# Two early one-row stores cut to a quarter of a row each, in a DMA-bound RMSNorm kernel

## The chip, the cores and the metric

The kernel runs on one core of a Trainium2 chip. The metric is the device time of one execution in microseconds. Before the change it is 162.1 us (median of 3 runs, 161.9 to 162.29).

## The reference

```python
x: (16, 1024, 512) float32, gamma: (512,) float32 (ones)
rms = np.sqrt(np.mean(x ** 2, axis=-1, keepdims=True) + 1e-5)
return (x / rms * gamma).astype(np.float32)
```

x has 33.55 MB and the output as many. Nothing can be left out: 67.1 MB cross between HBM (the chip's main memory) and SBUF (the core's working memory, in 128 partitions).

## The kernel before

The 16,384 rows are four tiles of 128 partitions x 32 rows. A partition's 32 rows lie one after the other in HBM (64 KB), so that a DMA is 128 contiguous runs, one per partition. Three buffers of a tile's size ("slots") hold tiles 0, 1, 2; tile 3 goes into slot 0 again. ScalarE (ACT) squares rows, VectorE (DVE) reduces some of them and applies scale and gamma in place. Every load and store of x and the output goes through one queue, issued by SyncE (SP) in the order of the program:

```python
def load(t, slot, r0, r1):
    nc.sync.dma_start(out=slots[slot][:, r0:r1], in_=xv[t][:, r0:r1])

def store(t, slot, r0, r1):
    nc.sync.dma_start(out=ov[t][:, r0:r1], in_=slots[slot][:, r0:r1])

load(0, 0, 0, 8)
load(0, 0, 8, 32)
# ... gamma to all partitions; row_stats (squares, sum, 1/rms) and apply (x * rstd * gamma), 8 rows at a time

def transfers(t, g):          # called after rows g..g+8 of tile t are applied
    if (t, g) == (0, 0):
        store(0, 0, 0, 1)     # early store 1: row 0, 2,048 B per partition
        load(1, 1, 0, 32)
        load(2, 2, 0, 16)
        store(0, 0, 1, 2)     # early store 2: row 1
        load(2, 2, 16, 32)
    elif (t, g) == (0, 24):
        store(0, 0, 2, 16)    # the "first big store"
        store(0, 0, 16, 32)
        load(3, 0, 0, 16)
        load(3, 0, 16, 32)
    # ... stores of tiles 1, 2, and of tile 3 in two halves
```

The statistics of a group are computed one group ahead of its application.

## Time and profile before

| | before |
|---|---|
| time, median | 162.1 us |
| span of the profiled run | 160.4 us |
| DVE, ACT busy | 76%, 50% |
| DMA queue, share of 16 engines' span | 97.7% |
| first packet of x starts, last packet ends | 1.74, 159.25 us |

These are lines of the page of the kernel before: the span, the busy times, the DMA share of 40 slices of the span, the count of packets (one packet is one partition's run; besides, each of the 15 DMAs of x and the output ends on every engine with a completion packet of 4 B, 240 of the 241 under 512 B), and the queue of all x and output traffic.

```profile
span 160.4 us, 410 instructions
PE 2.0 (1%) x2; PEld 0.5 (0%) x2; DVE 122.6 (76%) x163; ACT 80.1 (50%) x162; POOL 0.2 (0%) x4
...
DMA  5999999699699999999999999998998998999993
...
DMA packets 2164, 67.13 MB, mean 419 GB/s; under 512 B 241, under 2 KB 241, under 8 KB 498
...
q1 hardware_dynamic: 2160, 67.11, 97.7%
```

The DMA engines are the limit. No compute engine is near its own. The two slices with a 6 are no holes: long packets are counted where they start, and the packet records show the queue served in the order of issue without a gap. The 257 packets of at least 2 KB but under 8 KB are the 2 x 128 of the early stores and gamma.

The chain of waits names DVE, and this is the reading to be careful with. Here are its shares, and then the waits of the queue that issues the DMAs.

```profile
DVE 67%; DMA 13%; ACT 7%; issue 2%; DVEq 0%; SPq 0%
...
SPq L45 <- DVE slot L88: 97.9, 7, 29.8
SPq L42 <- DMA out_dram<-slot: 31.3, 2, 21.9
```

The last store is issued when DVE ends its last row, so the chain goes from there back through DVE. But an issued store stands in line. The packet records say that the last store, issued at 146.25 us, has its first packet at 148.28, behind the store before it. DVE is 2.0 us early even there.

### The profile page before, as it was taken

How to read it: one execution, taken by the hardware profiler on the slowest of the kernel's cores; microseconds unless marked ns; L12 is line 12 of the kernel's file. 1: busy time of each engine (PE TensorE's matmuls, PEld its weight loads, DVE VectorE, ACT ScalarE, POOL GpSimd, SP SyncE). 2: the span in 40 equal slices, each digit the busy share in tenths (PEclk: the TensorE clock that was granted, in tenths of full speed). 3: DMA queues.
4: the chain of work that ended last, by engine and by line, in shares of the span. 5: the costliest groups of instructions: out<-in, count | busy, mean ns of one | idle time of the engine just before them, and what ended most of it. 6: DMA issues, size and time to landing. Idle time of an engine off the chain costs nothing.

```text
span 160.4 us, 410 instructions
## 1 busy us (share of the span) xinstructions
PE 2.0 (1%) x2; PEld 0.5 (0%) x2; DVE 122.6 (76%) x163; ACT 80.1 (50%) x162; POOL 0.2 (0%) x4
## 2 busy tenths in 40 slices
PE   4000000000000000000000000000000000000000
PEld 1000000000000000000000000000000000000000
DVE  0100928999999519999999999999999999994000
ACT  3098039990390999996900950079609940000000
POOL 0000000000000000000000000000000000000000
DMA  5999999699699999999999999998998998999993
GB/s 197 523 392 392 466 449 523 261 523 523 262 402 387 455 458 418 453 415 466 409 392 498 409 400 507 409 507 376 425 507 360 441 507 360 417 400 441 449 417 147
DMA packets 2164, 67.13 MB, mean 419 GB/s; under 512 B 241, under 2 KB 241, under 8 KB 498
## 3 DMA queue, kind: packets, MB, share of 16 engines
q1 hardware_dynamic: 2160, 67.11, 97.7%
q14 instruction: 2, 0.02, 0.0%
q10 hardware_dynamic: 2, 0.00, 0.0%
HBM read 33.56 MB, written 33.55 MB: 418 GB/s over the span
## 4 chain that ended last, share of the span: by engine, by line
DVE 67%; DMA 13%; ACT 7%; issue 2%; DVEq 0%; SPq 0%
DVE slot L88 48%; DVE ss L71 18%; DMA slot<-in_x_dram 13%; ACT sq_scratch L76 3%; ACT sq L70 3%; DVE rstd L83 1%; DVEq L154 0%; ACT rms L82 0%; SPq L42 0%
## 5 line engine op out<-in xcount | busy, mean ns | idle before, releaser
L88 DVE SCALAR_TENSOR_TENSOR slot<-slot,rstd,gamma_b 128x512 f32<-128x512 f32 x128 | 85.8, 738 | 0.1
L76 ACT ACTIVATE sq_scratch<-slot 128x512 f32<-128x512 f32 x64 | 40.0, 625 | 10.0 <-DMA slot<-in_x_dram 8.7
L70 ACT ACTIVATE sq<-slot 128x2048 f32<-128x2048 f32 x16 | 29.8, 1864 | 18.6 <-DVE ss L71 11.5
L71 DVE TENSOR_REDUCE ss<-sq 128x4 f32<-128x2048 f32 x16 | 35.9, 2274 | 3.4 <-ACT sq L70 3.4
L82 ACT ACTIVATE rms<-ss,eps_t 128x8 f32<-128x8 f32 x16 | 4.6, 297 | 25.9 <-DVE ss L71 25.7
L83 DVE RECIPROCAL rstd<-rms 128x8 f32<-128x8 f32 x16 | 3.1, 193 | 16.1 <-ACT rms L82 16.1
L76 ACT ACTIVATION_READ_ACCUMULATOR sq_scratch<-slot 128x1 f32 x64 | 11.9, 186 | 0.0
L57 DVE COPY gamma_b<-sq 128x512 f32<-128x512 f32 x1 | 0.7, 691 | 3.3 <-PE sq L55 3.3
L55 PE MATMUL sq<-gamma_row,ones_col 1*128 1x512 f32 x2 | 2.0, 1122 | 2.2 <-DMA gamma_row<-in_gamma_dram 2.2
L76 ACT ACT_TABLE_LOAD x1 | 1.3, 1283 | 1.3 <-PEq L143 1.3
L82 ACT ACT_TABLE_LOAD x1 | 1.3, 1283 | 0.0
L53 DVE MEMSET ones_col<- 1x128 f32 x1 | 0.2, 165 | 0.8 <-PEq L143 0.8
L55 PEld LDWEIGHTS sq<-gamma_row,ones_col 1*128 1x128 f32 x2 | 0.5, 306 | 2.2 <-issue 2.2
L143 POOL MEMSET const-bfloat16-1.0<- 128x1 bf16 x1 | 0.1, 101 | 0.0
L143 POOL MEMSET const-uint8-127<- 128x1 uint8 x1 | 0.1, 101 | 0.0
L143 POOL MEMSET const-float32-0.0<- 128x1 f32 x1 | 0.1, 98 | 0.2 <-issue 0.2
L143 POOL MEMSET const-float32-1.0<- 128x1 f32 x1 | 0.1, 98 | 0.0
L60 DVE MEMSET eps_t<- 128x1 f32 x1 | 0.1, 59 | 0.0
## 6 DMA issues: line engine op xcount, KB each, us to landing
slot<-in_x_dram SPq DMA_DIRECT2D x4, 4096.0 KB, 27.6
out_dram<-slot SPq DMA_DIRECT2D x3, 4096.0 KB, 18.8
slot<-in_x_dram SPq DMA_DIRECT2D x1, 6144.0 KB, 21.5
out_dram<-slot SPq DMA_DIRECT2D x1, 3584.0 KB
slot<-in_x_dram SPq DMA_DIRECT2D x1, 2048.0 KB, 7.2
out_dram<-slot SPq DMA_DIRECT2D x2, 256.0 KB, 21.3
out_dram<-slot SPq DMA_DIRECT2D x2, 29.8
gamma_row<-in_gamma_dram ACTq DMA_DIRECT2D x1, 2.0 KB
```

Source lines behind the costliest of these rows:

```text
L53: nc.vector.memset(ones_col, 1.0)
L55: nc.tensor.matmul(gamma_psum[:, 0], ones_col, gamma_row, start=True, stop=True)
L57: nc.vector.tensor_copy(out=gamma_b, in_=gamma_psum[:, 0])
L60: nc.vector.memset(eps_t, eps)
L70: nc.scalar.activation(out=sq, in_=slots[slot][:, g + h : g + h + H, :], func=AF.Square)
L71: nc.vector.tensor_reduce(out=ss[:, h : h + H], in_=sq, axis=mybir.AxisListType.X, op=OP.add)
L76: nc.scalar.activation(out=sq_scratch, in_=slots[slot][:, g + r, :], func=AF.Square, accum_out=ss[:, r : r + 1],)
L82: nc.scalar.activation(out=rms, in_=ss, func=AF.Sqrt, bias=eps_t, scale=1.0 / D)
L83: nc.vector.reciprocal(out=rstd, in_=rms)
L88: nc.vector.scalar_tensor_tensor(out=slots[slot][:, g + r, :], in0=slots[slot][:, g + r, :], scalar=rstd[:, r : r + 1], in1=gamma_b, op0=O ...
L143: nc = _bacc.Bacc("TRN2", target_bir_lowering=False, num_devices=1)
```

## The change

The idea: the two early stores are made as small as a quarter of a row (512 B per partition), so that they take less of the queue from the loads behind them. The first big store takes the rest. Nothing else changes.

```diff
+    def store_elements(t, slot, e0, e1):
+        nc.sync.dma_start(
+            out=ov[t].rearrange("p r d -> p (r d)")[:, e0:e1],
+            in_=slots[slot][:].rearrange("p r d -> p (r d)")[:, e0:e1],
+        )
...
-            store(0, 0, 0, 1)
+            store_elements(0, 0, 0, D // 4)
             load(1, 1, 0, 32)
             load(2, 2, 0, 16)
-            store(0, 0, 1, 2)
+            store_elements(0, 0, D // 4, D // 2)
             load(2, 2, 16, 32)
...
-            store(0, 0, 2, 16)
+            store_elements(0, 0, D // 2, 16 * D)
```

## The prediction

> **What bounds the kernel now.** The 16 DMA engines. The page puts the DMA queue at 97.7% of the engines' span, 67.1 MB at 419 GB/s. The trace's packet records show one queue, served in issue order, with no hole: the first packet of x starts at 1.74 us, the last ends at 159.25, the span is 160.4. The longest packets (65,536 B, 2.418 us) give 27.1 GB/s per engine, at which its 4.19 MB take 154.8 us: the 157.5 us of DMA hold some 2.7 us of overhead. The Trainium skill ("DMA: Bandwidth & Descriptors", Specifications) puts the fabric ceiling at 435 GB/s; 16 x 27.1 = 434 agrees.
>
> The chain of waits names DVE for 67%, because the last store is issued when DVE ends its last row (146.25 us in the timeline). But its first packet starts only at 148.27, behind the store before it. DVE is 2.0 us ahead of the queue here, 3.4 at tile 2's store, 7.5 or more elsewhere.
>
> **What the change does.** No instruction is added or removed. The two early stores go from 128 packets of 2,048 B each to 128 of 512 B; the 393 KB taken from them go into the first big store of slot 0 (28,672 to 31,744 B per partition). A 2,048 B packet took 84 ns, against 75.6 at the rate above: 8 ns of overhead. If that is fixed, a 512 B packet takes an estimated 27 ns; each engine has 16: 0.43 us in place of 1.34. The big store's packets grow by 0.113 us, 8 per engine: +0.91. The sum is zero. If a 512 B write costs as much as a 2,048 B one (the same skill section puts the least size for line rate at 512 B, so this is its edge), the sum is +0.9; I expect 0.0 to +0.3.
>
> What moves: tile 1 lands some 0.45 us earlier (42.7 to 42.3), tile 2's second half 0.9 earlier, until the big store gives it back near 72 us. ACT waits 3.3 us for tile 1, but then again for DVE's reductions to free PSUM (to 52.0 us), so this is absorbed. The second early store now depends on row 0 alone; it was issued at 17.99, after row 1 was done, so this buys nothing.
>
> **On the critical path:** only packet overhead, near zero. I predict 162.1 us, with 8 chances in 10 for 161.5 to 163.0. Faster by over 2%: 0.01; within 2%: 0.95; slower by over 2%: 0.04. (2% is 3.2 us.)
>
> **What would show it.** Right: packets under 2 KB rise by 256, those under 8 KB stay; DMA share stays at 97 to 98%; 512 B packets take 25 to 40 ns; tile 1 lands 0.3 to 0.6 us earlier; from the store of slot 0's second half on, all is within 0.5 us of before. Wrong in cost: 512 B packets take 80 ns or more. Wrong in hiding: a hole in the DMA queue before a late store.
>
> **What would make it wrong.** ACT and DVE interleave row groups (single-row and four-row squares alternate), so the order seems chosen at build time, perhaps from assumed DMA times. Another order could end DVE later: by over 2 us to show, by over 5 to cost 2%. DVE stands idle 5.4 us before 59.6; an order could add to that. I give a changed order 40%, a harmful one 8%. An earlier DVE end cannot help: the queue is full.

## More of the kernel before

The order of instructions on ACT and DVE is chosen when the program is built.

## The result, and the profile after

After: 162.7 us median (162.47 to 162.97, 4 runs); before, with the runs of that round, 162.12 us (161.9 to 162.29, 4 runs). The ratio is 1.0038, 95% interval 1.0014 to 1.0062. A ratio is the mean time of one kernel's fast runs over that of the other's of the same rounds, so it is not quite the ratio of the medians. By the 2% rule the two are the same; but the two sets of four do not overlap, and the change costs about 0.6 us.

The same lines of the page of the kernel after:

```profile
span 161.1 us, 411 instructions
PE 2.0 (1%) x2; PEld 0.5 (0%) x2; DVE 122.6 (76%) x163; ACT 80.1 (50%) x162; POOL 0.2 (0%) x4
...
DMA  5999999969999999999999999899899799799992
...
DMA packets 2164, 67.13 MB, mean 417 GB/s; under 512 B 241, under 2 KB 497, under 8 KB 498
...
q1 hardware_dynamic: 2160, 67.11, 97.5%
...
DVE 64%; DMA 13%; ACT 10%; issue 2%; DVEq 0%; SPq 0%
```

Compute is the same to a tenth of a microsecond, the packets are as many, and 256 of them have moved under 2 KB. Apart from line numbers, the sizes of three DMAs and one more semaphore wait on DVE (at 114.98 us; with it the page counts 411 instructions, and DVE still ends 0.18 us sooner), the built programs have the same instructions in the same order on every engine. The DMA queue is as full as before and 0.7 us longer.

Where do the 0.7 us arise? The DMA view of a narrow window, taken at the issue of one DMA, has a line for that DMA (and at times one for its neighbour): its size, where it is given, and the time from issue to landing. These lines are tile 1's load, the second half of tile 2's, the store of the second half of tile 0, and the last store. First before (line 2 was issued at 18.51, line 3 at 49.81, line 4 at 146.25 us):

```profile
slot<-in_x_dram SPq DMA_DIRECT2D x1, 25.7
...
slot<-in_x_dram SPq DMA_DIRECT2D x1, 4096.0 KB, 44.9
...
out_dram<-slot SPq DMA_DIRECT2D x1, 4096.0 KB, 32.1
...
out_dram<-slot SPq DMA_DIRECT2D x1, 4096.0 KB, 13.3
```

Then after (issued at 18.50, 49.62, 146.07 us):

```profile
slot<-in_x_dram SPq DMA_DIRECT2D x1, 25.0
...
slot<-in_x_dram SPq DMA_DIRECT2D x1, 4096.0 KB, 44.4
...
out_dram<-slot SPq DMA_DIRECT2D x1, 4096.0 KB, 32.8
...
out_dram<-slot SPq DMA_DIRECT2D x1, 4096.0 KB, 14.2
```

Tile 1 lands 0.7 us earlier (predicted: 0.3 to 0.6). The second half of tile 2, which should have been 0.9 us early, is only 0.5 early. Then the big store takes back its 0.9 us, as it had to, and everything behind it is late by 0.5 us or more. So time was gained ahead of the first early store and more was lost in the loads of tile 2.

The DMA view of two windows finds it. Only packets that *start* in the window are counted, with their full duration, so a share can exceed 100%; share x window x 16 / packets is the mean duration of a packet. First before, 19.8 to 20.4 us (the last packet of each engine ahead of early store 1), then 58.2 to 61.5 us (the last packets of tile 2's load, ahead of the first big store):

```profile
q1 hardware_dynamic: 16, 0.79, 350.2%
...
q1 hardware_dynamic: 46, 1.51, 106.2%
```

Then after, the same two windows:

```profile
q1 hardware_dynamic: 16, 0.79, 302.9%
...
q1 hardware_dynamic: 32, 1.05, 101.2%
```

In the first window the 49,152 B packets took 2.10 us before (3.502 x 0.6 us) and 1.82 after; such a packet takes 1.815 us when undisturbed. In the second the 32,768 B packets took 1.22 us before (1.062 x 3.3 x 16 / 46) and 1.67 after; undisturbed, 1.213. So *loads* become slow just ahead of a store, and the change has moved this from the early stores to the big one.

To compare runs I sum, over the packets of a stretch, the duration less size / 27.1 GB/s, and divide by 16. The result is the lost time per engine. A small store's own packets are included: 128 of 2,048 or of 512 B have 8 ns each over the rate, which is 0.06 us per engine. The last two columns are the mean and the latest start of the last store's 16 completion packets.

| trace | lost up to early store 1's end | from there up to early store 2's | up to the big store's start | sum | queue's end, mean | slowest engine |
|---|---|---|---|---|---|---|
| before | 0.38 us | 0.45 | 0.08 | 0.90 | 158.34 us | 159.24 |
| after | 0.08 | 0.15 | 0.97 | 1.20 | 158.74 | 159.98 |

The first column starts at the end of the first load; the second leaves out tile 1's load (0.03 to 0.04 us). The sum rises by 0.30 us. The queue's mean end rises by 0.40 (0.05 of it is there when the first load ends), and the slowest engine, which sets the span, by 0.74: its lag on the mean is 1.24 us in place of 0.90.

The table leaves out one more place. Ahead of the store of tile 1, where the queue turns from loads to stores again, the last packets of tile 3's load are slow too. Here are the 16 packets that start at 98.7 to 99.9 us before, the 16 at 98.9 to 100.1 us after, and the last one of the slowest engine after (100.1 to 100.2 us):

```profile
q1 hardware_dynamic: 16, 0.52, 112.2%
...
q1 hardware_dynamic: 16, 0.52, 110.5%
...
q1 hardware_dynamic: 1, 0.03, 112.9%
```

Their means are 1.35 and 1.33 us in place of 1.213, and the single one took 1.81 us (1.129 x 0.1 x 16). This second loss is smaller, some 0.03 to 0.19 us per engine over all traces, but uneven: by the completion packets, the lag of the slowest engine grew from 0.65 to 0.92 us there before, and from 0.79 to 1.25 after (in the repeats below from 0.58 to 0.83 and from 0.71 to 1.05).

### The profile page after: what moved, and what is told of

Read it like the earlier page. It is cut to its first block, busy times and chain, and to the rows that moved or that the text cites. A ratio compares the mean times of both kernels' runs of the same rounds, so it can differ in the third digit from the quotient of the medians.

```text
span 161.1 us, 411 instructions
## 1 busy us (share of the span) xinstructions
PE 2.0 (1%) x2; PEld 0.5 (0%) x2; DVE 122.6 (76%) x163; ACT 80.1 (50%) x162; POOL 0.2 (0%) x4
## 3 DMA queue, kind: packets, MB, share of 16 engines
q1 hardware_dynamic: 2160, 67.11, 97.5%
## 4 chain that ended last, share of the span: by engine, by line
DVE 64%; DMA 13%; ACT 10%; issue 2%; DVEq 0%; SPq 0%
DVE slot L94 45%; DVE ss L77 18%; DMA slot<-in_x_dram 13%; ACT sq_scratch L82 5%; ACT sq L76 5%; DVE rstd L89 1%; ACT rms L88 1%; DVEq L160 0%; SPq L42 0%; DVEq L94 0%
## 5 line engine op out<-in xcount | busy, mean ns | idle before, releaser
L76 ACT ACTIVATE sq<-slot 128x2048 f32<-128x2048 f32 x16 | 29.8, 1864 | 18.9 <-DVE ss L77 12.0
```

Source lines behind the costliest of these rows:

```text
L76: nc.scalar.activation(out=sq, in_=slots[slot][:, g + h : g + h + H, :], func=AF.Square)
```

## The experiments

Eleven kernels ran. Theory A: the changed big store itself (where its rows start, or its length) makes the loads ahead of it slow. Theory B: the early stores used to take this stall in advance, and became too small for it. Each kernel keeps the order of instructions on DVE and ACT unless said otherwise, and each gave the right result. The diffs are against the changed kernel where not said otherwise.

### The two kernels once more

No edit.

> Control: the changed kernel once more. If the 0.6 us are real and come from the last two load packets of each engine ahead of the first big store (they took about 1.75 and 1.6 us in place of 1.213 between 58 and 62 us), the time is 162.5 to 162.9 us and the trace shows the same slow packets, some 0.9 us per engine, in the same place. Rival: those slow packets were a chance of one execution; then they are gone or elsewhere, and the time is not tied to them.

> Control: the kernel before, profiled once more. If the trace's stalls belong to the program, its load packets are slow just ahead of the two early stores again (0.3 to 0.4 us per engine each, near 20 and 49.5 us) and not ahead of the first big store (under 0.1 us); time 162.1 +- 0.2. Rival (chance): the stalls lie elsewhere or have other sizes.

After: 162.68 us (162.25 to 163.05, 6 runs). Before, as a kernel of its own: 162.00 us (161.87 to 162.16, 6 runs). The shared runs of before on this chip scattered more (162.2, 161.85 to 163.53, 11 runs), so that the ratio of after is 1.0021 with an interval of 0.9992 to 1.005. Over all rounds the 43 runs of before have a median of 162.13, the 10 of after 162.68. I take the cost as 0.5 to 0.6 us; the interval of the second comparison alone would not show it.

The stalls came again. After: 0.12, 0.10, 0.92 us, with the slow packets at the same place. Before: 0.51, 0.10, 0.36. So in before the stall at early store 1 came both times, but the second part was paid at early store 2 in one execution and ahead of the big store in the other; there I had expected under 0.1. The sum is steady: 0.97 (0.90 before), and 1.15 (1.20) after.

### The big store as it was, with one small early store

```diff
-            store_elements(0, 0, D // 4, D // 2)
+            store_elements(0, 0, D // 4, 2 * D)
-            store_elements(0, 0, D // 2, 16 * D)
+            store_elements(0, 0, 2 * D, 16 * D)
```

> First early store 512 B per partition as in the change, second takes the rest of rows 0 and 1 (3,584 B), so that the big store has the 28,672 B at byte 4,096 that it had before. Theory A (the changed big store itself, its start or length, makes the loads ahead of it slow): no slow packets near 58 to 62 us, time at or a little under that of before, 161.8 to 162.2. Rival B (small early stores merely move a stall to a later store): the slow packets ahead of the big store stay, time 162.5 to 162.8.

162.62 us (162.09 to 163.05). Lost: 0.09, 1.09, 0.06 us. Nothing is lost ahead of the big store, as theory A said, but the time did not come back: the whole stall now lies ahead of the second early store, which has 3,584 B per partition. So neither expectation was right as written. The stall goes to the first store that is not small.

### The long big store, with whole early rows

```diff
-            store_elements(0, 0, 0, D // 4)
+            store_elements(0, 0, 0, D)
-            store_elements(0, 0, D // 4, D // 2)
+            store_elements(0, 0, D, 2 * D)
-            store_elements(0, 0, D // 2, 16 * D)
-            store(0, 0, 16, 32)
+            store_elements(0, 0, 2 * D, 2 * D + 31 * D // 2)
+            store_elements(0, 0, 2 * D + 31 * D // 2, 32 * D)
```

> Early stores of one row each as before; the big store starts at byte 4,096 as before but has 31,744 B as after, and the store behind it is that much shorter. Theory A by length: loads slow ahead of the big store by some 0.9 us per engine, time 162.5 or more. Theory A by start (byte 1,024 in the changed kernel): no slow packets there, time 162.1. Rival B: no slow packets there, time 162.1.

162.12 us (161.95 to 162.18). Lost: 0.44, 0.12, 0.36 us, sum 0.92: the pattern of before. The length of the big store does not matter. Together with the run above this leaves theory A nothing that it explains; its start at byte 1,024 was not tried alone.

Theory C replaces A and B: the loads ahead of the first stores lose a roughly fixed time, nearly all of it once in a run; the sizes of the first stores decide where, and whether in one piece or two.

### Four sizes of the early stores

half_row: 1,024 B each. two_rows: 4,096 B each. first_full: row 0, then a quarter of row 1. no_early: both deleted, the big store has rows 0 to 16.

```
 half_row     store_elements(0, 0, 0, D // 2)   store_elements(0, 0, D // 2, D)      big: D .. 16 * D
 two_rows     store_elements(0, 0, 0, 2 * D)    store_elements(0, 0, 2 * D, 4 * D)   big: 4 * D .. 16 * D
 first_full   store_elements(0, 0, 0, D)        store_elements(0, 0, D, 5 * D // 4)  big: 5 * D // 4 .. 16 * D
 no_early     (none)                            (none)                               big: 0 .. 16 * D
```

> Two early stores of half a row, 1,024 B per partition each. Theory C (once in a run, the first stores of some size make the loads ahead of them slow, some 0.7 to 1.0 us per engine in total; a store that is too small doesn't trigger it and leaves it to the next; going up from 512 B, with no stall, to 2,048 B, with 0.35 us): stalls of 0.05 to 0.2 us per engine at the early stores, 0.6 to 0.9 us ahead of the big store; time 162.3 to 162.7 us. Rival D (it is the length or start of the big store that counts): its rows start at byte 2,048; a stall only if that is unlucky too, no graded picture.

> Two early stores of two rows, 4,096 B per partition each. Theory C: all of the stall, 0.9 to 1.1 us per engine, at the first early store near 20 us, under 0.15 us at the second and ahead of the big store; time 162.3 to 162.7 us, slower than before although the early stores are larger. Rival (larger early stores are always better, the change was bad because it made them smaller): under 162.1 us. The build also orders three instruction groups differently after 110 us; DVE is ahead of the DMA queue there, so it should not show.

> Only the second early store is a quarter of a row; the first is a whole row as before. Theory C: 0.35 us per engine at the first, nothing at the second, 0.3 to 0.6 us ahead of the big store; time 162.0 to 162.3, near before. If each of the two early stores has its own share in the gain: 162.3 to 162.5.

> No early stores at all; the big store has 16 whole rows. Theory C: nothing near 20 and 50 us, 0.9 to 1.0 us per engine ahead of the big store, and 0.1 us per engine less overhead of small packets: 162.4 to 162.7 us, as the changed kernel. Rival (each change of direction of the queue costs, the two early stores cost something): under 162.0 us.

| kernel | time, median (range), 6 runs | ratio to before (95% interval) | lost: 1st, 2nd, big | sum |
|---|---|---|---|---|
| half_row | 162.40 (162.17 to 162.98) | 1.0007 (0.9986 to 1.0028) | 0.19, 0.56, 0.43 us | 1.19 us |
| two_rows | 162.73 (162.33 to 162.89) | 1.0019 (1.0002 to 1.0037) | 1.01, 0.09, 0.06 | 1.16 |
| first_full | 162.17 (161.92 to 162.49) | 0.9987 (0.997 to 1.0004) | 0.44, 0.09, 0.46 | 0.98 |
| no_early | 162.64 (162.36 to 163.53) | 1.0028 (1.0003 to 1.0052) | 0.01, 0.07, 1.29 | 1.37 |

two_rows, first_full and no_early came out as theory C said, in place, and in time to 0.03 us. no_early lost 1.29 us ahead of the big store, where 0.9 to 1.0 was expected. Larger early stores are no better than smaller ones: 4,096 B take all of it at 20 us. half_row is a miss in place: I had expected at most 0.2 us at its second store and 0.6 to 0.9 ahead of the big store, and it lost 0.56 and 0.43. Differences of 0.2 us in time are within the scatter of these runs; the sums are one trace each.

### Which part of a store sets it off: reading SBUF, or writing HBM?

In sbuf_copy a copy inside SBUF stands in early store 1's place; in dram_copy a copy inside HBM. Early store 2 has 512 B in both, and the big store stores everything that is still missing or wrong.

```diff
 sbuf_copy
-            store_elements(0, 0, 0, D // 4)
+            nc.sync.dma_start(out=slots[2][:, 0:2], in_=slots[0][:, 0:2])
 dram_copy
-            store_elements(0, 0, 0, D // 4)
+            nc.sync.dma_start(out=ov[0][:, 0:2], in_=xv[0][:, 0:2])
```

> In the place of the first early store stands a copy inside SBUF, 4,096 B per partition from slot 0 to slot 2 (overwritten later by tile 2); the second early store has 512 B; the big store has all the rest. The copy adds 4,096 B x 8 / 27.1 GB/s = some 1.2 us of DMA per engine. What two_rows paid at once (1.0 us per engine ahead of a first 4,096 B store) comes either from reading store data out of SBUF (theory E) or from writing to HBM (theory F). E: loads slow by 0.8 to 1.1 us per engine ahead of the copy near 20 us, and under 0.2 ahead of the big store. F: nothing ahead of the copy, 0.8 to 1.0 ahead of the big store. Time 163.5 to 164.2 either way; the place of the stall tells.

> In the place of the first early store stands a copy inside HBM, 4,096 B per partition's rows from x to the output (rows 0 and 1 of tile 0, wrong values that the big store overwrites later, so the result is right); the second early store has 512 B; the big store has 16 whole rows. Theory F (writing to HBM is what costs once): 0.8 to 1.1 us per engine of slow packets at the copy, under 0.2 ahead of the big store. Theory E (reading from SBUF): nothing unusual at the copy, 0.8 to 1.2 us ahead of the big store. Time 163.3 to 164.5 either way.

Here are the same two windows of sbuf_copy, 19.8 to 20.4 and 58.2 to 61.5 us:

```profile
q1 hardware_dynamic: 12, 0.59, 337.3%
...
q1 hardware_dynamic: 47, 1.54, 108.0%
```

And of dram_copy, 19.8 to 20.4 and, since its copy moved things by 1 us, 59.4 to 62.1 us:

```profile
q1 hardware_dynamic: 16, 0.79, 302.5%
...
q1 hardware_dynamic: 32, 1.05, 131.0%
```

In sbuf_copy the load packets ahead of the copy took 2.70 us (3.373 x 0.6 x 16 / 12) in place of 1.815, and those ahead of the big store the undisturbed 1.213. In dram_copy it is the other way round: 1.815 ahead of the copy, 1.77 ahead of the big store in place of 1.213. The lost times are 1.31, 0.09, 0.06 us and 0.06, 0.14, 1.17 us. A DMA that reads SBUF and writes no HBM takes the stall; one that writes HBM and reads no SBUF does not. This is clear-cut for theory E, in one trace each. The two copies differ in one more thing: dram_copy's waits for nothing and was issued at 1.62 us, sbuf_copy's at 17.14. That a store issued long ahead can still take the stall is seen in the changed kernel: its big store was issued at 36.75 us, and the loads ahead of it were slow at 58 to 62. The times, 163.62 us (5 runs) and 164.21 us (4 runs), include the added bytes and say nothing about it.

### One early store

```diff
-            store_elements(0, 0, 0, D // 4)
+            store_elements(0, 0, 0, D)
-            store_elements(0, 0, D // 4, D // 2)      (deleted)
-            store_elements(0, 0, D // 2, 16 * D)
+            store_elements(0, 0, D, 16 * D)
```

> One early store of one row, no second one. Theory C: 0.35 to 0.45 us per engine at it, nothing near 50 us, 0.3 to 0.5 us ahead of the big store; time 161.9 to 162.2 us, as before or a trace better for 8 packets per engine less. If the second early store of the kernel before earns something: 162.3 or more.

162.16 us (162.02 to 162.32), ratio 1.0001 (0.9981 to 1.0022). Lost: 0.61, 0.05, 0.28 us, sum 0.93. The place is right, the size at the early store was more than the expected 0.45. Within the scatter, the kernel before needs only one of its two early stores, of a whole row. No version beat the kernel before clear of the scatter.

Over the eleven traces without an added copy, the sum lost runs from 0.90 to 1.37 us and the queue's mean end from 158.20 (first_only) to 158.92 us (no_early), with a correlation of 0.92.

## Why the prediction was right, and where it was off

The time, 162.7 us, lies in the stated range and within 2%, for the reason given: the queue is full, no bytes were added, and DVE stays ahead of it. That the range held the extra 0.6 us is owed to its width: the sum behind it has no term for what was lost.

- *512 B packets take an estimated 27 ns.* Right: 27 ns for 255 of the 256, 29 for the other. The fixed overhead of 8 ns holds at 2,048 and at 512 B.
- *Packets under 2 KB rise by 256, share 97 to 98%.* Right: 241 to 497, 97.5%.
- *The order of instructions may change (40%).* It did not; one semaphore wait was added on DVE.
- *A hole before a late store.* None; the last store was issued at 146.07 us and began at 148.52, so DVE's lead grew to 2.5 us.
- *The sum is zero, I expect 0.0 to +0.3.* Too small; about +0.5 to +0.6 was measured. The mis-sized term is one that the sum did not have: the time that loads lose ahead of the first stores (0.90 us per engine before, 1.20 after), and how unevenly the engines lose it. The prediction counted overhead per packet as if it were fixed, and never asked where the 2.7 us lay. A third of them, 0.90 us, could be read from the trace of before, among them load packets of 2.1 us in place of 1.815 just ahead of early store 1.
- *Tile 1 lands 0.3 to 0.6 us earlier; all later things are within 0.5 us.* Off for that cause: 0.7 us earlier, since the stall ahead of early store 1 went (0.38 to 0.08 us), then up to 0.74 us later at the end, since it came back larger (0.08 to 0.97) and the slowest engine's lag grew by 0.34.

Shown: the loss lies in load packets ahead of the first stores; nearly all of it is taken once; which store takes it depends on the stores' sizes; reading SBUF sets it off, writing HBM does not. This is not the whole cost: of the 0.74 us by which the slowest engine ends later, 0.40 are the later mean end (0.30 of it the larger sum) and 0.34 this engine's larger lag on the mean. Part of that lag comes ahead of tile 1's store, where it grew by 0.46 us after and by 0.27 before; why, no run tells.

Not shown is the mechanism. With 4 KB per engine in the first store, 0.08 to 0.12 us were lost ahead of it, with 16 KB 0.38 to 0.61, and with 32 KB 1.01; a loss of 1 us at 27.1 GB/s stands for an estimated 27 KB per engine. That looks as if so much of a store were read in advance, while the load is still under way, but this is a guess, and half_row speaks against it: the 8 KB per engine of its second store are an estimated 0.30 us at that rate, and 0.56 us were lost there, only 0.06 of them in the store's own packets. Still open: why the loss is less in two steps (0.90 to 0.98 us) than in one (1.15 to 1.37), why half_row lost 1.19 in three, and why the engines lag unevenly (the slowest by 1.24 and 1.03 us in the two traces of after, 0.90 and 0.81 before).

## What to carry to other kernels

When the DMA queue is full, compare single packets with their undisturbed duration, by place, instead of trusting the share: 97.7% hid a stall of 0.9 us, and the change moved and enlarged it at 97.5%. A small transfer may earn its place by what it does to its neighbours; before shrinking it for its own bytes, look at the packets ahead of it. And when the chain of waits ends in a store's issue, check from the packets whether that store was waited for at all.

## What the Trainium skill lacked or had wrong

- "DMA: Bandwidth & Descriptors" has nothing on loads that slow down, nearly all of it once in a run, ahead of the first DMAs of a queue that read SBUF: 0.9 to 1.4 us per engine in these runs, and 32,768 B packets of 1.67 us in place of 1.213.
- The same page, Specifications, gives 512 B as the least transfer for line rate. Here a 512 B packet of a store took 27 ns, against 18.9 ns at the rate of the longest packets (512 B / 27.1 GB/s): 70% of it. A 2,048 B packet took 84 ns, 90%.
- The same section gives about 27 GiB/s per engine; 65,536 B in 2.418 us are 27.1 GB/s, which is 25.2 GiB/s. Its fabric ceiling of 435 GB/s agrees with 16 x 27.1 = 434.
